# One quarter of s multiplied a pair of products earlier, and four buffers for the gates of att in the last za pair

## The chip, the cores and the metric

The kernel runs on one core of a Trainium2 chip. The metric is the device time of one execution in microseconds (us); the median of the runs shown counts. The core has five engines that run side by side, each in the order of its own instruction list: PE (TensorE: matrix products into PSUM), DVE (VectorE) and ACT (ScalarE: elementwise work), POOL (GpSimd, here mainly an issuer of DMAs) and SP (SyncE, an issuer of DMAs). An instruction that waits holds up whatever stands behind it on its engine; for SP and POOL that is the DMAs queued there.

## The reference

One layer of a streaming encoder with 1024 tokens and a width of 1024. What the change touches is the gate path of the attention branch and the merge of the spatial-gating branch:

```
q, k, v, za, u, vs, zs, gm = split(rmsnorm(x) @ w_in)
a   = window_sink_attention(q, k, v, att_sinks)
a   = (a * silu(za)) @ w_att_out
sgo = chunked_spatial_gating(gelu(u), gelu(vs), ...)
sgo = (sgo * silu(zs)) @ w_sg_out
ga, gs = split(sigmoid(gm + b_merge))
y   = ga * a + gs * sgo
out = rmsnorm(x + y @ w_o)
```

In the kernel's names, `at_dr` holds the attention's result, `a_dr` is `a * silu(za)`, `z_dr` holds `zs` before its silu, `s1_dr` the spatial gating's result that it is multiplied with, and s is their product `silu(zs) * s1`. `gs_dr` and `ga_dr` hold the two halves of `gm`. These are scratch tensors in DRAM, 1024 by 1024 f32.

## The kernel before, in words

**Products.** Every large product is done in pairs of 128-row blocks by `gemm_pair` (from line 345 on): a pair is cut in quarters and made with seven products of half size instead of eight. Each product (`product`, the matmuls of line 342) is 4 times 3 matmuls of 128 by 512, as each f32 operand is split in a high and a low part: ACT casts the high part (`split`, line 155) and DVE subtracts to get the low part (line 156). The right-hand operand is kept as seven forms, named b11, t1, t2, b21, t3, b22, t4 in the order of use; each form has one buffer for its high and one for its low part, so a form for the next stage can be filled once the current stage has used it for the last time. Weights go through `wr` or `s` into `wh` and `wl`, three buffers each (`split_next`). PSUM holds `acc` (tag `ps_mm`), which takes b11, then t2, t3 and t4 on top of one another; between them ACT or DVE must have read it: the copy of line 360 after b11, the copy of line 367 after t2, the subtraction of line 377 after t3. Lines 364, 372 and 381 take the others.

**Hooks.** `gemm_pair` calls a hook after each of its seven products, so other work can be interleaved by hand. The hooks are numbered 1 to 7; (m, h) below is hook h of the pair that begins at block m, with m = 0, 2, 4, 6.

**The za stage.** Four pairs multiply the normalised input's forms with the za weights. Each quarter of a result (`finish`, line 1561) goes through a silu on ACT, and a hook later `finish_silu` multiplies it on DVE (line 1540) with the quarter of att that it gates, `gates.pop(0)`, stores it with a DMA from POOL (line 458) and asks for another gate with `want_gate`, a load of 256 KB from `at_dr` on SP. There are 16 such gates. In this stage they use two buffers, `g0` and `g1`; two gates are asked for at the start and each product asks for the next but one. `finish_silu` runs at hooks 1, 5, 6 and 7, one result behind, and once more after the stage.

**Making s in the shadow of za.** `parts_of_s` (line 1474 on) is a table from (m, h) to steps that prepare the four quarters of s in four buffers `bq0` to `bq3`. A step can load a quarter of `z_dr` (1 MB), apply the silu in place (two ACT instructions, line 1500), load the factors of `s1_dr`, or multiply. Two quarters, those with j = 0, are multiplied with a whole quarter of factors in `bq0` (line 1504). The other two, (1, 1) and (1, 0), are multiplied row by row (line 1511), four rows each, with row loads of 256 KB in buffers `g2` and `g3`. Quarter (1, 0) comes last: its own buffer is `bq0`, which is free only when the second half of quarter (0, 1) has been multiplied at (2, 7). Silus are placed behind the last copy out of PSUM on ACT (`pace`), multiplies behind the last addition on DVE (`term`); these are orders on an engine and not waits. Within such orders and the data's own waits, the compiler's scheduler writes each engine's list.

**The passage to the s stage.** Before the last za pair the first combination of quarters is made (`forms_of`, line 185); after it the forms of s are filled, b11 first. Form b21 is quarter (1, 0); t3 and t4 are combinations, t4 with quarter (1, 0) too. Four gates of `gs_dr` are asked for, in all four buffers, and the s pairs begin; there a gate gets its sigmoid on ACT (line 1574) and multiplies the results on DVE (lines 1581 and 1583).

Of the kernel before, what the change touches and what calls it, by code (L numbers as in the profile page):

```python
# [52 lines left out]
def hybrid_tile(  # L53
# [16 lines left out]
    nc = tc.nc  # L70
# [15 lines left out]
    def mtile(shape, dt, tag, bufs, pool=None):  # L86
        return (pool or main).tile(shape, dt, name=nm(tag), tag=tag, bufs=bufs)

    def scratch(name, shape=(D, S)):
        return dram.tile(list(shape), F32, name=name)  # L90
# [35 lines left out]
    at_dr = scratch("at_dr")  # L126
# [31 lines left out]
    def after(second, first):  # L158

        tc.add_manual_dep(  # L160
            second.ins,
            first.ins.name,
            mybir.DependencyInfo(mybir.DependencyClass.NoSync, mybir.DependencyReason.DATA),
            reason="order",
        )
# [33 lines left out]
    def copy_to(dst, src):  # L199
        nc.sync.dma_start(dst, src)  # L200
# [31 lines left out]
    def half_of(half):  # L232
        return slice(half * HALF, (half + 1) * HALF)
# [96 lines left out]
    term = [None]  # L330
# [20 lines left out]
    def gemm_pair(b, finish, hook=lambda: None, second="o"):  # L351

        n = done[0]
        done[0] += 1
        acc = bank("mm")[:]
        x11, x12, x22 = xtile(), xtile(), xtile()
        product(acc, ready[n, 0], b["b11"], True)
        pace[0] = nc.scalar.copy(x11[:], acc)  # L360
        hook()
        t5 = bank("o")[:]
        product(t5, ready[n, 2], b["t1"], True)
        pace[0] = nc.scalar.mul(x22[:], t5, -1.0)
        hook()
        product(acc, ready[n, 3], b["t2"], False)
        pace[0] = nc.scalar.copy(x12[:], acc)
        split_next()
        hook()
        t2 = bank(second)[:]  # L370
        product(t2, ready[n, 1], b["b21"], True)
        term[0] = term_of_x11[0] = nc.vector.tensor_add(x11[:], x11[:], t2)
        finish(0, 0, x11, x11[:], 1.0)
        split_next()
        hook()
        product(acc, ready[n, 4], b["t3"], False)
        term[0] = nc.vector.tensor_sub(x22[:], x22[:], acc)  # L377
        finish(1, 1, x22, x22[:], 1.0)
        hook()
        product(t5, ready[n, 5], b["b22"], False)  # L380
        term[0] = nc.vector.tensor_add(x12[:], x12[:], t5)
        finish(0, 1, x12, x12[:], 1.0)
        split_next()
        hook()
        product(acc, ready[n, 6], b["t4"], False)
        finish(1, 0, xtile(), acc, -1.0)
        split_next()
        hook()
# [65 lines left out]
    def place(dst, m, half):  # L454
        return dst[m * P : (m + 1) * P, half_of(half)]

    def put(dst, m, half, src, queue=nc.sync):
        queue.dma_start(place(dst, m, half), src)

    def get(src, m, half, bufs, tag="g"):  # L460
        g = mtile([P, HALF], F32, tag, bufs, pool)
        copy_to(g[:], place(src, m, half))
        return g
# [478 lines left out]
    for m in range(0, KC, 2):  # L942

        def finish(i, half, q, src, sign, m=m):
            nc.scalar.activation(q[:], src, AF.Gelu, scale=sign)
            late.append(lambda: mix(m + i, half, q))
# [448 lines left out]
    def bq(n=None):  # L1395
        if n is None:
            n_bq[0] += 1
        return mtile([P, 4, HALF], F32, f"bq{(n_bq[0] if n is None else n) % 4}", 1, pool)
# [47 lines left out]
    def forms_of(qs):  # L1446
        q11, q12, q21, q22 = (qs[k] for k in QUARTERS)
        b = {}

        def fill(name, q):  # L1450
            b.update(new_b((name,)))
            fill_b(b, name, q)

        combine(nc.vector.tensor_sub, q12, q11, q12)
        yield
        fill("b11", q11)
        fill("t1", q12)
        combine(nc.vector.tensor_add, q12, q22, q12)
        fill("t2", q12)
        fill("b21", q21)  # L1460
        combine(nc.vector.tensor_sub, q11, q12, q11)
        fill("t3", q11)
        fill("b22", q22)
        combine(nc.vector.tensor_sub, q21, q12, q21)
        fill("t4", q21)
        yield b

    ORDER = ((0, 0), (1, 1), (0, 1), (1, 0))
    gates = []

    turn = [0]

    def gtag(among=4):
        turn[0] += 1
        return f"g{turn[0] % among}"

    def want_gate(src, m, half, among=4):
        gates.append(get(src, m, half, 1, gtag(among)))

    def parts_of_s():  # L1480

        factors, of_rows = [], {}

        def rows(src, j, half):
            return src[:].rearrange("(c p) t -> p c t", p=P)[:, 4 * j : 4 * j + 4, half_of(half)]

        def load(j, half):
            s_q[j, half] = q = bq()  # L1490
            copy_to(q[:], rows(z_dr, j, half))

        def load_factors(j, half):
            factors.append(bq(0))
            copy_to(factors[-1][:], rows(s1_dr, j, half))

        def silu(j, half):
            for c in range(0, 4, 2):
                v = s_q[j, half][:, c : c + 2, :]
                after(nc.scalar.activation(v, v, AF.Silu), pace[0])  # L1500

        def multiply(j, half, c):
            v = s_q[j, half][:, c : c + 2, :]
            after(nc.vector.tensor_mul(v, v, factors[-1][:, c : c + 2, :]), term[0])

        def load_row(c, half):
            of_rows[c, half] = get(s1_dr, 4 + c, half, 1, f"g{2 + c % 2}")

        def multiply_row(c, half):
            v = s_q[1, half][:, c, :]  # L1510
            after(nc.vector.tensor_mul(v, v, of_rows[c, half][:]), term[0])

        return {
            (0, 1): [(load, 0, 0), (load_factors, 0, 0)],
            (0, 2): [(load, 1, 1)],
            (0, 3): [(load, 0, 1)],
            (0, 4): [(load_row, 0, 1), (load_row, 1, 1)],
            (0, 5): [(silu, 0, 0)],
            (0, 6): [(multiply, 0, 0, 0)],
            (0, 7): [(multiply, 0, 0, 2), (load_factors, 0, 1), (silu, 1, 1)],  # L1520
            (2, 1): [(multiply_row, 0, 1), (multiply_row, 1, 1), (load_row, 2, 1), (load_row, 3, 1)],
            (2, 3): [(silu, 0, 1)],
            (2, 6): [(multiply, 0, 1, 0), (multiply_row, 2, 1)],
            (2, 7): [(multiply, 0, 1, 2), (multiply_row, 3, 1), (load, 1, 0), (load_row, 0, 0), (load_row, 1, 0)],
            (4, 6): [(silu, 1, 0)],
            (4, 7): [(multiply_row, 0, 0), (multiply_row, 1, 0), (load_row, 2, 0), (load_row, 3, 0)],
            (6, 6): [(multiply_row, 2, 0), (multiply_row, 3, 0)],
        }


    of_att = [(m + i, half) for m in range(0, KC, 2) for i, half in ORDER]
    s_q = {}
    making_s = parts_of_s()
    of_za = [0]

    silus = []

    def finish_silu(q, m, half):

        after(nc.vector.tensor_mul(q[:], q[:], gates.pop(0)[:]), term[0])  # L1540
        put(a_dr, m, half, q[:], nc.gpsimd)
        if of_att:
            want_gate(at_dr, *of_att.pop(0), 2)

    def part_of_s(m):
        of_za[0] += 1
        if of_za[0] % 7 not in (2, 3, 4) and silus:
            finish_silu(*silus.pop(0))
        for f, *args in making_s.get((m, (of_za[0] - 1) % 7 + 1), ()):
            f(*args)  # L1550

    for m in range(0, KC, 2):
        if m == 0:
            for _ in range(2):
                want_gate(at_dr, *of_att.pop(0), 2)
        if m == 6:
            s_forms = forms_of(s_q)
            next(s_forms)

        def finish(i, half, q, src, sign):  # L1560
            pace[0] = nc.scalar.activation(q[:], src, AF.Silu, scale=sign)
            silus.append((q, m + i, half))

        gemm_pair(hb, finish, lambda: part_of_s(m), "tp")
    finish_silu(*silus.pop(0))
    for i, half in ORDER:
        want_gate(gs_dr, i, half)
    sb_ = next(s_forms)

    def gate_of(src, m, i, half, col):  # L1570

        g = gates.pop(0)
        c = col + m + i
        gate = nc.scalar.activation(g[:], g[:], AF.Sigmoid, bias=bm_sb[:, c : c + 1])

        after(gate, pace[0])
        return g
# [130 lines left out]
    for p in range(4):  # L1708
        acc = bank("sc" if p < 2 else "mm")[:]
        x11 = mtile([P, HALF], F32, gtag(), 1, pool)  # L1710
        product(acc, ready[N_PAIRS + p, 0], ob["b11"], True)
        nc.scalar.copy(x11[:], acc)
        accs.append(acc)
        firsts.append(x11)
# [185 lines left out]
```

## Time and profile before

| what | us |
|---|---|
| median of 3 runs | 914.42 (913.27 to 915.49) |
| the profiled execution, whole | 915.36 |
| its span, first to last instruction | 913.6 |
| busy in the span: PE, DVE, ACT, POOL | 895.3, 696.7, 527.1, 141.9 |
| mean granted clock of TensorE | 0.995 |

The profile is of one execution. The span is what the trace covers; the execution's own time is 1.8 us longer. Times in rows are us from the start of the span, L and a number is a line of the kernel. In a timeline row stand start, duration, engine, line, operation, output<-inputs, shapes, count, and in brackets how long the engine was idle before and what ended that. In the chain of waits each row is a start, a duration and what the end of the program hung on in that time. PE's matmuls overlap, so that their durations add up to more than the time.

### The profile page before, as it was taken

The numbers are of one execution on the slowest core, as the hardware profiler recorded it, in microseconds if no ns is written. First come the engines' busy times: TensorE is split into PE (matmuls) and PEld (weight loads), VectorE is DVE, ScalarE is ACT, GpSimd is POOL, SyncE is SP. The second block draws the span as 40 slices with busy tenths as digits, with TensorE's granted clock in tenths as the row PEclk, the third lists the DMA queues.
The fourth block names the chain that finished last, engine by engine and source line by source line (L and its number), as shares of the span: only waits on it lengthen the run. The fifth ranks groups of instructions, "written<-read, shape, count | busy, mean of one in ns | idle before, by whom it ended". The sixth has DMA issues, their size and how long they took to land.

```text
span 913.6 us, 13183 instructions
## 1 busy us (share of the span) xinstructions
PE 895.3 (98%) x4284; PEld 745.1 (82%) x4284; DVE 696.7 (76%) x1263; ACT 527.1 (58%) x1058; POOL 141.9 (16%) x204
## 2 busy tenths in 40 slices
PE   8999999999999899999999999999998999999996
PEld 6778888888888788888888888888877887888885
DVE  6869966666685678888878888647797589579996
ACT  6866533334544467677677676664674385367443
POOL 1222222212030001111110111201001111110012
PEclk9999999999999999999999999999999999999999
DMA  9997888958788657878686789899859755998632
GB/s 330 204 248 212 271 203 173 172 158 257 260 258 274 199 167 212 212 153 208 180 227 228 234 240 229 215 338 343 304 195 363 224 201 150 312 304 277 208 117 113
DMA packets 131598, 209.57 MB, mean 229 GB/s; under 512 B 12649, under 2 KB 61033, under 8 KB 131530
## 3 DMA queue, kind: packets, MB, share of 16 engines
q1 hardware_dynamic: 110072, 149.74, 49.7%
q0 software_dynamic: 21312, 58.73, 28.3%
q8 instruction: 34, 0.56, 0.3%
q14 instruction: 34, 0.28, 0.1%
q10 hardware_dynamic: 146, 0.27, 0.1%
HBM read 147.74 MB, written 86.11 MB: 256 GB/s over the span
## 4 chain that ended last, share of the span: by engine, by line
PE 88%; DVE 7%; DMA 2%; issue 1%; ACT 1%; SPq 0%; DVEq 0%; ACTq 0%
PE ps_mm L342 37%; PE ps_o L342 27%; PE ps_sc L1230 3%; PE ps_mm L669 3%; PE ps_tp L342 3%; PE ps_tp L669 2%; PE ps_o L1315 2%; PE ps_sc L342 2%; PE ps_tp L1274 2%; PE ps_o L669 2%; PE ps_tp L917 2%; PE ps_sc L669 1%; DVE bq L185 1%; DVE wl L156 1%; DMA wr<-in_w_dram 1%
## 5 line engine op out<-in xcount | busy, mean ns | idle before, releaser
L155 ACT CAST wh<-s 128x1024 fp32r<-128x1024 f32 (+1 forms) x79 | 79.2, 1005 | 90.2 <-PE ps_mm L342 48.6
L156 DVE TENSOR_TENSOR wl<-wr,wh 128x512 fp32r<-128x512 f32 (+1 forms) x77 | 72.0, 936 | 51.3 <-ACT wh L155 50.7
L156 DVE TENSOR_TENSOR wl<-s,wh 128x1024 fp32r<-128x1024 f32 (+1 forms) x79 | 92.5, 1171 | 10.8 <-ACT wh L155 10.6
L155 ACT CAST wh<-wr 128x512 fp32r<-128x512 f32 (+1 forms) x77 | 63.1, 821 | 62.6 <-PE ps_mm L342 34.2
L342 PE MATMUL ps_o<-T_t1h,wh 128*128 128x512 f32 x148 | 58.9, 398 | 0.8 <-ACT wh L155 0.7
L342 PE MATMUL ps_o<-T_b22h,wh 128*128 128x512 f32 x148 | 58.2, 393 | 0.0
L342 PE MATMUL ps_o<-T_b22l,wh 128*128 128x512 f32 x148 | 57.9, 391 | 0.0
L342 PE MATMUL ps_o<-T_b22h,wl 128*128 128x512 f32 x148 | 57.8, 390 | 0.0
L342 PE MATMUL ps_mm<-T_b11h,wl 128*128 128x512 f32 x140 | 54.9, 392 | 2.8 <-DVE wl L156 2.8
L342 PE MATMUL ps_o<-T_t1h,wl 128*128 128x512 f32 x148 | 57.7, 390 | 0.0
L342 PE MATMUL ps_o<-T_t1l,wh 128*128 128x512 f32 x148 | 57.6, 389 | 0.0
L342 PE MATMUL ps_mm<-T_t4h,wh 128*128 128x512 f32 x140 | 55.5, 397 | 1.2 <-DVE x L377 1.2
L342 PE MATMUL ps_mm<-T_t2h,wl 128*128 128x512 f32 x140 | 55.2, 395 | 0.0
L342 PE MATMUL ps_mm<-T_t3l,wh 128*128 128x512 f32 x140 | 54.6, 390 | 0.6 <-DVE T_t3l L156 0.6
L342 PE MATMUL ps_mm<-T_t2l,wh 128*128 128x512 f32 x140 | 55.2, 394 | 0.0
L342 PE MATMUL ps_mm<-T_t4h,wl 128*128 128x512 f32 x140 | 55.1, 394 | 0.0
L342 PE MATMUL ps_mm<-T_b11h,wh 128*128 128x512 f32 x140 | 55.1, 393 | 0.0
L342 PE MATMUL ps_mm<-T_t4l,wh 128*128 128x512 f32 x140 | 55.0, 393 | 0.0
L342 PE MATMUL ps_mm<-T_t2h,wh 128*128 128x512 f32 x140 | 55.0, 393 | 0.0
L342 PE MATMUL ps_mm<-T_b11l,wh 128*128 128x512 f32 x140 | 54.9, 392 | 0.0
L342 PE MATMUL ps_mm<-T_t3h,wh 128*128 128x512 f32 x140 | 54.9, 392 | 0.0
L1243 ACT ACTIVATE pr<-ps_sc,sm 128x192 f32<-128x192 f32 (+2 forms) x128 | 50.9, 410 | 6.6 <-DVE sm L1239 5.5
(389 smaller groups left out, 2397.4 us busy)
## 6 DMA issues: line engine op xcount, KB each, us to landing
wr<-in_w_dram SPq DMA_DIRECT2D x86, 256.0 KB
sums<-in_w_dram POOLq DMA_DIRECT2D x20, 512.0 KB, 6.5
s<-sums SPq DMA_DIRECT2D x20, 512.0 KB
q_hl<-qhl SPq DMA_DIRECT2D x16, 512.0 KB
q<-q_hl SPq DMA_DIRECT2D x64, 128.0 KB
y_dr<-x POOLq DMA_DIRECT2D x28, 256.0 KB, 6.7
g<-in_w_dram POOLq DMA_DIRECT2D x12, 512.0 KB, 6.7
wr<-in_w_dram SPq DMA_DIRECT2D x11, 512.0 KB
```

The costliest lines, as they stand in the source:

```text
L155: nc.scalar.copy(hi, src)
L156: return nc.vector.tensor_sub(lo, src, hi.bitcast(F32))
L185: op(dst[:, i : i + 2, :], a[:, i : i + 2, :], c[:, i : i + 2, :])
L342: nc.tensor.matmul(acc, lt, rt, start=fresh and k == 0 and n == 0, stop=k == 3 and n == 2, skip_group_check=True,)
L669: mm = nc.tensor.matmul(acc[:], lt, rt, start=fresh and k == 0 and n == 0, stop=k == 3 and n == 2, skip_group_check=True,)
L917: nc.tensor.matmul(pm[:, t * P : (t + 1) * P], xh[:, half * 4 + t, g * P : (g + 1) * P], bias[-1][1][:, g % 4, :], start=True, stop=True,)
L1230: nc.tensor.matmul(sc[:, i, k0:], q_of[:, c, i * P : (i + 1) * P], kt[:, f, k0:], start=f == 0, stop=f == 1,)
L1243: nc.scalar.activation(held_in[c, i], sc[:, i, lo:hi], AF.Exp, bias=nmax[:, c, i : i + 1], scale=-1.0, accum_out=sums[:, c, i : i + 1],)
L1274: nc.tensor.transpose(dst, pr[:, i, block * P : block * P + width], ident[:])
L1315: nc.tensor.matmul(po[:, cs], lt, rt, start=n == 0, stop=n == len(terms) - 1)
```

## The change

A list `free_tags` takes the place of the counter that named the gates' buffers. It begins with `g0` and `g1`; a gate takes the first free name and gives it back when it is used. At the start of the last za pair (m = 6) `g2` and `g3` are added and two more gates are asked for. For that, row loads in `g2` and `g3` have to be through: the steps for quarter (1, 0) are moved in the table.

| step for quarter (1, 0) | before | after |
|---|---|---|
| load of the quarter, loads of rows 0 and 1 | (2, 7) | (2, 7) |
| silu | (4, 6) | (4, 2) |
| multiplies of rows 0 and 1, loads of rows 2 and 3 | (4, 7) | (4, 3) |
| multiplies of rows 2 and 3 | (6, 6) | (4, 6) |

```diff
-    turn = [0]
-
-    def gtag(among=4):
-        turn[0] += 1
-        return f"g{turn[0] % among}"
-
-    def want_gate(src, m, half, among=4):
-        gates.append(get(src, m, half, 1, gtag(among)))
+    free_tags = ["g0", "g1"]
+
+    def gtag():
+        tag = free_tags.pop(0)
+        free_tags.append(tag)
+        return tag
+
+    def want_gate(src, m, half):
+        tag = free_tags.pop(0)
+        gates.append((tag, get(src, m, half, 1, tag)))
+
+    def next_gate():
+        tag, g = gates.pop(0)
+        free_tags.append(tag)
+        return g
...
-            (4, 6): [(silu, 1, 0)],
-            (4, 7): [(multiply_row, 0, 0), (multiply_row, 1, 0), (load_row, 2, 0), (load_row, 3, 0)],
-            (6, 6): [(multiply_row, 2, 0), (multiply_row, 3, 0)],
+            (4, 2): [(silu, 1, 0)],
+            (4, 3): [(multiply_row, 0, 0), (multiply_row, 1, 0), (load_row, 2, 0), (load_row, 3, 0)],
+            (4, 6): [(multiply_row, 2, 0), (multiply_row, 3, 0)],
...
-        after(nc.vector.tensor_mul(q[:], q[:], gates.pop(0)[:]), term[0])
+        after(nc.vector.tensor_mul(q[:], q[:], next_gate()[:]), term[0])
         put(a_dr, m, half, q[:], nc.gpsimd)
         if of_att:
-            want_gate(at_dr, *of_att.pop(0), 2)
+            want_gate(at_dr, *of_att.pop(0))
...
-        if m == 0:
+        if m in (0, 6):
+            if m:
+                free_tags += ["g2", "g3"]
             for _ in range(2):
-                want_gate(at_dr, *of_att.pop(0), 2)
+                want_gate(at_dr, *of_att.pop(0))
...
-        g = gates.pop(0)
+        g = next_gate()
```

## The prediction

> **What bounds the kernel now.** I read the page first, then the chain of waits, then each engine's timeline from 592 to 745 us, where the four za pairs and the first s pair lie.
>
> ```profile
> span 913.6 us, 13183 instructions
> ...
> PE 88%; DVE 7%; DMA 2%; issue 1%; ACT 1%; SPq 0%; DVEq 0%; ACTq 0%
> ```
>
> PE holds 88% of the chain, so time is won or lost where PE stands still or runs at a lower clock. The chain of waits leaves PE once near the change, at the passage from the za pairs to the s pairs:
>
> ```profile
> 670.78 5.11 DMA g<-at_dr
> ...
> 690.36 1.15 DVE wl L156
> 691.51 0.04 issue
> 691.55 6.90 PE ps_mm L342 x22
> ```
>
> Up to 691.55, where PE resumes, the chain runs through DVE, which prepares the forms of s and the next weights for PE, and through one DMA: the last gate of att, issued at 670.78, 5.11 us. The same in DVE's timeline (start, duration, line, out<-in, idle time before):
>
> ```profile
> 657.95 2.36 DVE L156 TENSOR_TENSOR T_t1l<-bq,T_t1h 128x1024 fp32r<-128x1024 f32 x2 [0.36 <-ACT T_t1h L155]
> 670.64 1.29 DVE L1511 TENSOR_TENSOR bq<-bq,g 128x512 f32<-128x512 f32 x2
> 675.98 0.69 DVE L1540 TENSOR_TENSOR x<-x,g 128x512 f32<-128x512 f32 x1 [1.01 <-DMA g<-at_dr]
> ```
>
> After 657.95 DVE has hardly an idle moment up to 691.5. In it stand the two row multiplies of line 1511 (1.29 us) and one idle time of 1.01 us, for that gate. What PE loses by it is in the table of windows (PE busy, PEld, DVE, ACT, POOL, clock, DMA share, GB/s):
>
> ```profile
> 680.67:698.29 17.62, 14.51 (x54) 10.67 (x54) 16.76 (x19) 9.89 (x12) 1.62 (x3) 0.90 0.81 294
> 689.20:692.57 3.37, 1.63 (x6) 1.03 (x7) 3.37 (x5) 0.45 (x1) 0.17 (x1) 1.00 1.04 377
> 692.57:695.98 3.41, 3.41 (x9) 2.63 (x8) 3.41 (x6) 0.00 (x0) 1.45 (x3) 0.50 1.07 392
> 764.00:778.00 14.00, 12.84 (x56) 9.98 (x54) 13.06 (x16) 5.89 (x7) 3.51 (x4) 1.00 0.49 132
> ```
>
> In 17.62 us PE is busy for 14.51, so 3.1 us are idle, 1.74 of them in the 3.37 us before 692.57. Then the granted clock is 0.50 for 3.41 us, which costs half of that, 1.7 us.
>
> **The change part by part.** (a) The multiplies of rows 2 and 3 of quarter (1, 0) leave hook 6 of the last za pair (670.64) for hook 6 of the pair before (about 648). (b) The silu of that quarter moves from hook 6 to hook 2 of that pair, its first two row multiplies from hook 7 to hook 3, and with them the loads of rows 2 and 3. (c) Buffers g2 and g3, free by then, take two att gates at the start of the last pair. (d) Buffer names come from a free list, which elsewhere gives the same first-in, first-out order. No instruction is added or removed; all are moved.
>
> **Gain on DVE.** The two multiplies take 1.29 us out of the full stretch. The wait of 1.01 us goes too. SP now issues the 15th gate at 666.14 and the 16th at 670.78, each when the product two before has freed one of two buffers:
>
> ```profile
> 666.14 0.33 SPq L200 DMA_DIRECT2D g<-at_dr  x1
> ```
>
> With four buffers gates 14 and 15 go out when g2 and g3 come free, and the last one behind the 12th product at 652.88; all three have over 10 us before their use after 670, twice the 5.11 us that the chain shows for the last. So DVE can be 2.3 us earlier at 691.5. ACT bounds this from below:
>
> ```profile
> 678.98 1.05 ACT L155 CAST T_t3h<-bq 128x1024 fp32r<-128x1024 f32 x1 [2.96 <-DVE bq L185]
> 679.93 0.58 ACT L367 COPY x<-ps_mm 128x512 f32<-128x512 f32 x1
> ```
> ```profile
> 639.87 0.39 PE L342 MATMUL ps_tp<-T_b21h,wh 128*128 128x512 f32 x1
> ```
> ```profile
> 677.95 0.39 PE L342 MATMUL ps_tp<-T_b21h,wh 128*128 128x512 f32 x1
> ```
>
> ACT waits 2.96 us for DVE at 678.98 and is then never idle until the next wait of the passage. The copy at 679.93 (line 367) follows the t2 product, after which PE starts b21 at 677.95; two pairs earlier the same copy comes at 640.37 (row below), half a microsecond behind b21's start at 639.87, so this one can move 1.5 us. The casts around it can pass it, since the written order goes by readiness. Bounds 1.5 and 2.3 us; I take 2.2, nearer to DVE's row, the one the chain names.
>
> PE would then resume at 691.55 - 2.2 = 689.35. It also reaches that wait earlier: the stalls ahead of it (3.1 - 1.74 = 1.4 us) shrink as well. A single stop of 1.6 to 1.9 us is left, about as long as now, so I leave the half-clock stretch where it is.
>
> The Trainium skill (TensorE: Matmul & The Clock Gate, "What's actually happening") says that the clock is halved after at least one idle window of about 3.4 us. The length of the stretch agrees with it, the cause does not: here 1.74 idle us in 3.37 were enough. By the page's rule there would be no half-speed stretch either before or after and nothing to win from it; by the rows, 1.7 us.
>
> **Cost of the early silu.** The quarter is loaded at 637.07, after the multiply that frees its buffer; this load isn't moved:
>
> ```profile
> 608.74 3.04 SPq L200 DMA_DIRECT2D g<-at_dr  x2
> 637.07 0.37 SPq L200 DMA_DIRECT2D bq<-z_dr  x1
> ```
> ```profile
> 637.34 0.60 ACT L364 ACTIVATE x<-ps_o 128x512 f32<-128x512 f32 x1 [2.13 <-PE ps_o L342]
> 639.84 0.62 ACT L155 CAST wh<-wr 128x512 fp32r<-128x512 f32 x1 [1.90 <-PE ps_mm L342]
> 640.37 0.58 ACT L367 COPY x<-ps_mm 128x512 f32<-128x512 f32 x1
> 646.23 0.63 ACT L1561 ACTIVATE x<-x 128x512 f32<-128x512 f32 x1 [2.09 <-DVE x L377]
> 649.53 2.00 ACT L1500 ACTIVATE bq<-bq 128x1024 f32<-128x1024 f32 x2
> ```
>
> Hook 2 lies at 637.34 (the line 364 scaling), so the silu may be queued any time after 637.9. Its 1 MB isn't there yet. Bounds from the nearest rows: the gate issued last of the two from 608.74 on ended waits of DVE at 619.56 and after, behind 1 MB loads, and the one issued at 649.54 (second of two) at 652.88:
>
> ```profile
> 619.56 1.36 DVE L1540 TENSOR_TENSOR x<-x,g 128x512 f32<-128x512 f32 x2 [0.60 <-DMA g<-at_dr]
> 652.88 0.69 DVE L1540 TENSOR_TENSOR x<-x,g 128x512 f32<-128x512 f32 x1 [0.42 <-DMA g<-at_dr]
> 630.60 0.69 DVE L1540 TENSOR_TENSOR x<-x,g 128x512 f32<-128x512 f32 x1 [0.73 <-ACT x L1561]
> 632.35 1.22 DVE L1504 TENSOR_TENSOR bq<-bq,bq 128x1024 f32<-128x1024 f32 x1
> ```
> ```profile
> 646.82 3.05 SPq L200 DMA_DIRECT2D g<-at_dr  x2
> ```
> ```profile
> 620.67 0.43 SPq L200 DMA_DIRECT2D bq<-s_dr  x1
> ```
>
> That is 3.3 to 10.8 us, so the quarter lands between 640.4 and 647.9. The order that the compiler wrote narrows it. ACT works in order, and behind a silu that waits stand the copy at 640.37, the casts of the next pair's weights and the silus of za. Where it is queued decides. The order seems to know how late loads are: the multiply at 632.35 needs the 1 MB issued at 620.67, and DVE idled 0.73 us before 630.60 without it, so it was not expected before 630, over 9 us after its issue. The same 9 us after 637.07 give 646, my estimate of the landing, and the silu lies beside the za silu at 646.23. There ACT has 2.09 us of idle time before and the 2.00 us that the silu leaves free at 649.53, and the cost is nothing. If that cover is gone the price is that of the rivals: bounds 0 and 8.4 us (arrival at 647.9, ahead of the copy).
>
> The Trainium skill (DMA: Bandwidth & Descriptors, "Anatomy of one DMA — SWDGE (gpsimd) path") fits 2.0 us plus bytes over 436 GB/s, an estimate of 4.4 us for 1 MB, with the landing at 641.5. By that the silu would wait for almost nothing wherever it is queued; the gates above took up to 10.8 us for a quarter of the bytes.
>
> **The moved loads and multiplies.** The first two row multiplies need half of the silu, so they run near 647 instead of 651.17, beside these:
>
> ```profile
> 642.59 0.39 PE L342 MATMUL ps_mm<-T_t3h,wh 128*128 128x512 f32 x1
> 648.02 0.39 PE L342 MATMUL ps_mm<-T_t4h,wh 128*128 128x512 f32 x1
> ```
> ```profile
> 645.50 0.69 DVE L377 TENSOR_TENSOR x<-x,ps_mm 128x512 f32<-128x512 f32 x1 [0.63 <-PE ps_mm L342]
> 651.17 1.28 DVE L1511 TENSOR_TENSOR bq<-bq,g 128x512 f32<-128x512 f32 x2
> 655.23 2.36 DVE L156 TENSOR_TENSOR T_b11l<-bq,T_b11h 128x1024 fp32r<-128x1024 f32 x2 [0.53 <-ACT T_b11h L155]
> ```
>
> Line 377 at 645.50 frees the bank that PE's t4 product (648.02) adds into; it must not be late by more than 1.8 us. After them SP issues rows 2 and 3, near 648.4 instead of 651.98:
>
> ```profile
> 651.98 0.86 SPq L200 DMA_DIRECT2D g<-s_dr  x2
> ```
>
> At 3.3 to 10.8 us they land at 651.7 to 659.2. Up to 655.23 the two multiplies fit in the room left by line 1511 at 651.17 and the idle 0.53: no cost. If they land after 657.95 they fall into the full stretch and 1.3 us of the gain is gone. The nearest row, 649.54, gives 3.3 us, so I count nothing. Loads queued behind them on SP (the gates, the sums of weights) keep number and size and two gates move from 666 and 670 to about 654.
>
> **Sum.** Against the profiled execution: 913.6 us span plus 1.8 around it is 915.36, and 0.9 above the median of 914.42. It loses 2.2, with costs of nothing: 913.2 there, 912.2 on the median.
>
> **Rivals.** *The clock stays up.* If the stop is under some 1.2 us, or is cut by another order of the products, the 0.50 stretch goes. For: the passage at 764 to 778, of the same build, has 1.16 us idle (14.00 - 12.84) and a clock of 1.00. Against: I count a stop of 1.6 or more. 912.2 - 1.7 = 910.5.
>
> *The row multiplies stop DVE.* If the first two stand ahead of line 377, this waits for half the silu (646 + 1.0), two multiplies (1.28) and its own 0.69: done at 649.0, and t4 starts 1.0 us late, 3.0 if the next weights' cast is ahead too. 912.2 + 1.0 to 3.0: 913.2 to 915.2, about no change. For: they have the earlier place in the program. Against: they are ready only after 645.50.
>
> *The rows come late*, behind the sums on SP as the row at 651.98 would be, and the stretch keeps its 1.3 us: 913.5.
>
> *Slower: the silu is queued ahead of the copy at 640.37.* The copy must be done before PE's t3 product at 642.59, which adds to the bank it reads. With the load landing at L it is done at L + 2.00 + 0.53 + 0.58, so PE stands from L = 639.5 on, and from L = 641.7 the gain is used up. At L = 646, 6.5 us late: 912.2 + 6.5 = 918.7; at 644, 916.7. For: the program places it at hook 2, ahead of the copy. Against: the order at 632.35.
>
> **How the numbers follow.** Forecast 0.33; clock stays up 0.22; DVE stopped 0.15; rows late 0.14; slower 0.16. A difference counts from 0.2%, 1.8 us. Faster: 0.26 of the forecast (its own range, 911.5 to 913.2, reaches past 912.6), 0.22, and 0.04 from the rows' case, 0.52. Slower: 0.16 and 0.03 from the stopped DVE, 0.19. No change: the rest, 0.29. The range runs from 909.6 (2.3 gained, the clock up, a further 0.8 of stop gone) to 917.0; it leaves out the upper 0.10 of the slow case and little below.
>
> **What would show it.** Right: no idle DVE before line 1540 near 674, no line 1511 after 657, PE resuming about 2 us sooner than 691.55, the silu of line 1500 starting near 646. The clock: a 0.50 stretch after the passage or none. Wrong: a stop of PE near 642 or 648; ACT idle ahead of line 1500; row loads issued after 651; or a passage in which ACT's casts, not DVE, are what PE waits for.

## The result and the profile after

The changed kernel takes 915.65 us (median of 22 runs, 913.67 to 918.36) where the kernel before takes 913.99 in the same series (22 runs, 911.70 to 915.53): the ratio is 1.002, with a 95% interval of 1.0013 to 1.0028. It is slower by a little; the forecast was faster. The profiled execution of the changed kernel took 917.38 us, against 915.36 for that of before.

```profile
span 915.6 us, 13184 instructions
```

Lines from 1471 on have moved: the silu of a quarter is now L1507, the multiplies of a quarter L1511, the row multiplies L1518, the za multiply L1547, the za silu L1570. The matmuls and the lines up to 381 keep their numbers.

The passage from za to s, the place that the change is for, is better. The table of windows (length, then busy time of PE, PEld, DVE, ACT, POOL, then clock, DMA share, GB/s) after:

```profile
649.17:652.39 3.22, 0.00 (x1) 0.00 (x0) 2.11 (x4) 1.33 (x3) 0.00 (x0) 1.00 0.47 163
653.16:656.58 3.42, 3.42 (x9) 2.65 (x8) 3.32 (x5) 1.31 (x2) 1.08 (x2) 0.50 0.77 244
680.67:698.29 17.62, 16.45 (x72) 12.98 (x71) 17.62 (x20) 11.34 (x14) 1.01 (x2) 1.00 0.87 328
```

In the third row PE is idle for 1.17 us where it was 3.11 before, and the clock is 1.00 throughout. But the first two rows are new, 40 us ahead of the passage: PE does nothing for 3.22 us, and 0.77 us later its clock is halved for 3.41. PE's timeline names the place, between the last product of b22 and the first of t4 in the third za pair:

```profile
648.78 0.39 PE L342 MATMUL ps_o<-T_b22h,wl 128*128 128x512 f32 x1
652.39 0.50 PE L342 MATMUL ps_mm<-T_t4h,wh 128*128 128x512 f32 x1 [3.22 <-DVE x L377]
...
695.18 0.50 PE L342 MATMUL ps_mm<-T_b11h,wl 128*128 128x512 f32 x1 [0.94 <-DVE wl L156]
```

The last row is the longest stop that is left at the passage, 0.94 us. The chain of waits shows how the new stop comes about (start, duration, what the end hung on):

```profile
637.23 9.69 DMA bq<-z_dr
...
647.02 2.01 ACT bq L1507 x2
649.03 0.52 ACT x L1570
649.55 0.94 ACT wh L155
...
650.51 0.04 DVE wl L156
...
651.66 0.69 DVE x L377
...
652.39 1.87 PE ps_mm L342 x5
```

Read from the top: the load of quarter (1, 0) takes 9.69 us; the silu has been waiting for it; behind the silu stand the za silu and the cast `wh` of the next weights; behind the cast stands its low part on DVE; behind that L377, which frees the bank that t4 adds into. ACT's and DVE's timelines, with the idle time in brackets:

```profile
641.35 0.58 ACT L367 COPY x<-ps_mm 128x512 f32<-128x512 f32 x1
647.02 2.01 ACT L1507 ACTIVATE bq<-bq 128x1024 f32<-128x1024 f32 x2 [5.09 <-DMA bq<-z_dr]
648.93 0.61 ACT L1570 ACTIVATE x<-x 128x512 f32<-128x512 f32 x1
649.45 1.03 ACT L155 CAST wh<-wr 128x1024 fp32r<-128x1024 f32 x1
```
```profile
648.12 1.29 DVE L1518 TENSOR_TENSOR bq<-bq,g 128x512 f32<-128x512 f32 x2 [3.66 <-ACT bq L1507]
650.51 1.23 DVE L156 TENSOR_TENSOR wl<-wr,wh 128x1024 fp32r<-128x1024 f32 x1 [1.11 <-ACT wh L155]
651.66 0.68 DVE L377 TENSOR_TENSOR x<-x,ps_mm 128x512 f32<-128x512 f32 x1
```

In the kernel before the same cast ran 6.9 us earlier in the trace (5.9 if counted from the first za pair, which begins 1.0 us later in the changed kernel's trace). What it waited for was PE's b21 product, as the bracket says, and no load:

```profile
642.56 1.06 ACT L155 CAST wh<-wr 128x1024 fp32r<-128x1024 f32 x1 [1.61 <-PE ps_tp L342]
```

The account, counted from one matmul's start to the next beyond the usual 0.227 us: the third pair lost nothing and now loses 5.08 (3.38 of stop, 1.7 of half clock); the passage lost 5.78 (1.7 of them half clock) and now loses 1.72. That is +5.08 - 4.06 = +1.0; and in this execution the first za pair began 1.0 us later than in that of before, work which the change does not touch. Together they are the 2.0 us between the two spans. The medians differ by 1.66. That this is so near is in part luck, as the second 1.0 us is scatter: over the ten profiles of this document the first za pair begins between 592.2 and 594.7.

### The profile page after: what moved, and what is told of

It reads as the page before. It is cut to its first block, busy times and chain, and to the rows that moved or that the text cites. A ratio compares the mean times of both kernels' runs of the same rounds, so it can differ in the third digit from the quotient of the medians.

```text
span 915.6 us, 13184 instructions
## 1 busy us (share of the span) xinstructions
PE 896.0 (98%) x4284; PEld 745.9 (81%) x4284; DVE 696.4 (76%) x1263; ACT 527.2 (58%) x1058; POOL 141.3 (15%) x204
## 4 chain that ended last, share of the span: by engine, by line
PE 84%; DVE 8%; DMA 3%; issue 2%; ACT 2%; SPq 0%; DVEq 0%; ACTq 0%
PE ps_mm L342 35%; PE ps_o L342 26%; PE ps_sc L1230 3%; PE ps_mm L669 3%; PE ps_tp L669 2%; PE ps_o L1315 2%; PE ps_sc L342 2%; PE ps_tp L1274 2%; PE ps_tp L342 2%; PE ps_o L669 2%; PE ps_tp L917 2%; DVE wl L156 1%; DVE bq L185 1%; PE ps_sc L669 1%; DMA bq<-z_dr 1%
## 5 line engine op out<-in xcount | busy, mean ns | idle before, releaser
L342 PE MATMUL ps_mm<-T_t3h,wl 128*128 128x512 f32 x140 | 54.7, 390 | 0.0
```

Source lines behind the costliest of these rows:

```text
L342: nc.tensor.matmul(acc, lt, rt, start=fresh and k == 0 and n == 0, stop=k == 3 and n == 2, skip_group_check=True,)
```

## The experiments

The theory after the profile: the load lands 5 us after the place at which the written order has its silu, and the engines, which keep their order, pass this on through the cast to L377 and t4. The rival: the two row multiplies ahead of L377 are what stops t4. Each table below stands in place of the changed kernel's; ratios are to the kernel before, on the same chip in the same series. The changed kernel's 1.002 is of an earlier series; the first four experiments share one series and the last four another.

### The silu later: e1_silu_hook4

```diff
-            (4, 2): [(silu, 1, 0)],
-            (4, 3): [(multiply_row, 0, 0), (multiply_row, 1, 0), (load_row, 2, 0), (load_row, 3, 0)],
-            (4, 6): [(multiply_row, 2, 0), (multiply_row, 3, 0)],
+            (4, 4): [(silu, 1, 0)],
+            (4, 5): [(multiply_row, 0, 0), (multiply_row, 1, 0), (load_row, 2, 0), (load_row, 3, 0)],
+            (4, 7): [(multiply_row, 2, 0), (multiply_row, 3, 0)],
```

> The silu of quarter (1, 0) two hooks later than in the change, at (4, 4), its first two row multiplies at (4, 5), the last two at (4, 7); four gate buffers in the last pair as in the change. Theory (early silu): what the change loses is only that ACT waits 5.1 us for the quarter's load with the cast of the next weights behind it; here the silu stands behind the za silus of (0, 0) and (1, 1), so PE has no stop in the third za pair, and the passage to s stays as short as after the change (1.7 us of lost PE time instead of 5.8): about 4 us under before, ratio 0.9945 to 0.997. Rival (the passage was short only because PE came late to it): the passage goes back to 4 us or more of lost time and the ratio is 0.998 to 1.000. Rival (multiplies): they stop DVE here as well, ahead of line 381, and PE stops by 1 us or more in the third pair.

Measured: 911.86 us (12 runs), ratio 0.997 (0.9959 to 0.9981). ACT's timeline and the windows:

```profile
643.61 1.05 ACT L155 CAST wh<-wr 128x1024 fp32r<-128x1024 f32 x1 [1.61 <-PE ps_tp L342]
644.57 0.62 ACT L1570 ACTIVATE x<-x 128x512 f32<-128x512 f32 x1
645.75 2.01 ACT L1507 ACTIVATE bq<-bq 128x1024 f32<-128x1024 f32 x2 [0.56 <-DMA bq<-z_dr]
```
```profile
640.00:660.00 20.00, 20.00 (x90) 16.56 (x89) 15.44 (x19) 13.39 (x18) 2.16 (x4) 1.00 0.94 321
680.00:697.00 17.00, 15.82 (x69) 12.47 (x68) 17.00 (x19) 10.02 (x13) 2.17 (x4) 1.00 0.87 314
```

The cast is ahead of the silu again, PE is busy for all of the 20 us round the old stop, and the passage keeps what the change gave it: 1.18 us idle, clock 1.00. So the gain at the passage does not come from the delay ahead of it, and this version is faster than both kernels. The ratio is at the slow end of what was expected: the two profiles' passages differ by the 4 us of the theory, the medians by 2.7.

### The multiplies later, the silu as in the change: e2_rows_late

```diff
-            (4, 3): [(multiply_row, 0, 0), (multiply_row, 1, 0), (load_row, 2, 0), (load_row, 3, 0)],
-            (4, 6): [(multiply_row, 2, 0), (multiply_row, 3, 0)],
+            (4, 6): [(multiply_row, 0, 0), (multiply_row, 1, 0), (load_row, 2, 0), (load_row, 3, 0)],
+            (4, 7): [(multiply_row, 2, 0), (multiply_row, 3, 0)],
```

> The silu stays at (4, 2) as in the change, but the first two row multiplies go to (4, 6) and the last two to (4, 7). Theory (the cast behind the silu): DVE's line 377 waits for the low part of the next weights, that for the cast on ACT, that for the silu and its load; so PE's stop ahead of t4 in the third pair stays at 3 us or more with the half-speed stretch behind it, and the time is that of the change, ratio to before 1.000 to 1.003. Rival (the multiplies ahead of line 377 stop DVE, as the prediction had it): the stop falls under 1.5 us, the half-speed stretch goes, and the ratio is 0.995 to 0.998.

Measured: 918.05 us (9 runs), ratio 1.0042 (1.0028 to 1.0057), more than expected. ACT's timeline, and then DVE's, where nothing stands ahead of L377 now but the cast's low part:

```profile
644.61 2.01 ACT L1507 ACTIVATE bq<-bq 128x1024 f32<-128x1024 f32 x2 [4.69 <-DMA bq<-z_dr]
646.53 0.61 ACT L1570 ACTIVATE x<-x 128x512 f32<-128x512 f32 x1
647.04 1.03 ACT L155 CAST wh<-wr 128x1024 fp32r<-128x1024 f32 x1
```
```profile
648.11 1.22 DVE L156 TENSOR_TENSOR wl<-wr,wh 128x1024 fp32r<-128x1024 f32 x1 [5.66 <-ACT wh L155]
649.25 0.68 DVE L377 TENSOR_TENSOR x<-x,ps_mm 128x512 f32<-128x512 f32 x1
```

t4 starts at 649.98: 5.37 us after the silu, just as in the changed kernel (652.39 - 647.02), where the two multiplies are between. They cost nothing there, since the cast is what DVE waits for in the end; the rival falls. The stop here is 2.97 us with half a clock behind it, and the passage loses 2.8 us in place of 1.72: DVE waits 1.41 us at 659.25 for a load of the rows moved back, and one of their multiplies, at 660.99, falls into the stretch in which DVE is never idle. The profiled execution is the fastest of the nine (916.06), so it does not show all of what the median lost.

### The table without the two more gates: e3_table_only

```diff
-        if m in (0, 6):
-            if m:
-                free_tags += ["g2", "g3"]
+        if m == 0:
...
+    free_tags += ["g2", "g3"]
     for i, half in ORDER:
```

> The change's table, but two gate buffers to the end of the za stage as before. Theory (both parts shorten the passage): the stop of 3.4 us in the third pair stays; in the passage DVE waits for the last gate again, about 1 us, so PE loses 2.5 to 4.5 us there instead of 1.7, and the time is 1 to 3 us over the change's: ratio to before 1.003 to 1.005. Rival (the gates don't matter, the moved multiplies did it): as the change, 1.001 to 1.003.

Measured: 918.76 us (6 runs), ratio 1.0052 (1.0034 to 1.0069). In its profile t4 stops for 2.71 us, again 5.37 us behind the silu (644.86 to 650.23), and there is half a clock both there and at the passage, which loses 4.7 us:

```profile
694.60:698.00 3.40, 3.40 (x9) 2.63 (x9) 3.40 (x6) 0.00 (x0) 1.47 (x3) 0.51 1.04 387
```

With two buffers the passage keeps most of its old loss, and the ratio is 0.0032 or 2.9 us above the changed kernel's 1.002: with this table the two more gates are worth that.

### The gates without the table: e4_gates_only

```diff
+        def more_gates():
+            free_tags.extend(("g2", "g3"))
+            for _ in range(2):
+                want_gate(at_dr, *of_att.pop(0))
...
-            (4, 2): [(silu, 1, 0)],
-            (4, 3): [(multiply_row, 0, 0), (multiply_row, 1, 0), (load_row, 2, 0), (load_row, 3, 0)],
-            (4, 6): [(multiply_row, 2, 0), (multiply_row, 3, 0)],
+            (4, 6): [(silu, 1, 0)],
+            (4, 7): [(multiply_row, 0, 0), (multiply_row, 1, 0), (load_row, 2, 0), (load_row, 3, 0)],
+            (6, 1): [(multiply_row, 2, 0), (multiply_row, 3, 0), (more_gates,)],
...
-        if m in (0, 6):
-            if m:
-                free_tags += ["g2", "g3"]
+        if m == 0:
```

> Silu at (4, 6) and first row multiplies at (4, 7) as before; the last two row multiplies at (6, 1) instead of (6, 6), and then four gate buffers. Nothing waits for the quarter's load early, and the two multiplies stay inside DVE's full stretch. Theory (both parts): no stop in the third pair; the 1.0 us wait for the last gate goes and 1.3 us of multiplies stay, so the passage loses 1 us less: ratio 0.998 to 0.9995, and 1.7 us less again if the half-speed stretch goes too. Rival (the gates don't matter): ratio 0.9995 to 1.0005.

Measured: 916.21 us (12 runs), ratio 1.0015 (1.0001 to 1.0029), a miss. DVE's and PE's timelines show one new loss:

```profile
658.69 1.29 DVE L1523 TENSOR_TENSOR bq<-bq,g 128x512 f32<-128x512 f32 x2 [3.02 <-DMA g<-s_dr]
...
667.92 0.68 DVE L377 TENSOR_TENSOR x<-x,ps_mm 128x512 f32<-128x512 f32 x1
```
```profile
668.65 0.50 PE L342 MATMUL ps_mm<-T_t4h,wh 128*128 128x512 f32 x1 [2.20 <-DVE x L377]
...
692.16 0.50 PE L342 MATMUL ps_mm<-T_b11h,wl 128*128 128x512 f32 x1 [1.73 <-DVE wl L156]
```

L1523 is the row multiply here. DVE stands for 3.02 us at the loads of rows 2 and 3, which were issued at 651.30 and landed at 658.7; the forms of s and L377 of the fourth pair queue behind, and t4 of that pair stops for 2.36 us from start to start. It is the changed kernel's fault in another place: an instruction that waits for a load was put ahead of one that PE needs. The gates did in this profile what was expected of them: the passage loses 3.1 us, against 4.1 of stops in the kernel before, and here no half clock comes on top. The profiled execution (914.37 us) is faster than the median, and in it 2.36 lost and some 2.7 won at the passage come out even. What the median lost beyond that no profile shows. Half-speed stretches behind these two stops in other executions are the likely cause: the twelve runs reach from 913.84 us at a mean clock of 0.999 to 918.81 at 0.993.

### The cast first, the multiplies ahead of L377: e5_cast_first

```diff
+        if rows_first:
+            after(term[0], rows_first.pop())
...
+            (4, 4): [(silu, 1, 0), (multiply_row, 0, 0), (multiply_row, 1, 0), (load_row, 2, 0), (load_row, 3, 0)],
```

The first two lines stand behind L377; `rows_first` holds the second row multiply. The last line takes the place of the lines for (4, 2) and (4, 3).

> The silu of quarter (1, 0) stands behind the cast of the next weights on ScalarE, and the multiplies of rows 0 and 1 are kept ahead of L377 (the subtraction that frees the bank of t4) by an order of their own; gates as in the changed kernel. The theory (the stop of t4 came through the cast that stood behind the silu: silu 2.0, cast 1.0, low part 1.2 behind the load that lands at 646.9): the cast runs at about 642.6 again; the multiplies wait for the silu and L377 comes at about 649.4, so t4 stops for 0.7 to 1.4 us in place of 3.38 and the clock stays at 1.00 behind it; the passage from za to s keeps its 1.7 us of loss; ratio to the kernel before 0.996 to 0.9995. The rival (the two multiplies alone are what held t4): a stop of 3 us or more, half the clock behind it, ratio 1.001 or more.

Measured: 912.12 us (11 runs), ratio 0.9982 (0.9971 to 0.9993). The timelines of DVE (L1511 is the silu here, L1522 the row multiply and L379 the old L377) and of PE:

```profile
643.24 1.23 DVE L156 TENSOR_TENSOR wl<-wr,wh 128x1024 fp32r<-128x1024 f32 x1 [0.17 <-ACT wh L155]
647.21 1.29 DVE L1522 TENSOR_TENSOR bq<-bq,g 128x512 f32<-128x512 f32 x2 [2.75 <-ACT bq L1511]
648.43 0.68 DVE L379 TENSOR_TENSOR x<-x,ps_mm 128x512 f32<-128x512 f32 x1
```
```profile
649.16 0.50 PE L342 MATMUL ps_mm<-T_t4h,wh 128*128 128x512 f32 x1 [1.38 <-DVE x L379]
```

With the multiplies alone between the silu and L377, t4 starts 3.04 us after the silu (646.12 to 649.16) in place of 5.37, PE idles 1.38 us in place of 3.22, and the clock stays up. Counted from start to start the stop is 1.54, a little over the expected 1.4.

### Work for PE in the stop: e6_keep_warm

Twelve products that nothing reads are added to the changed kernel, between b22 and t4:

```diff
+        def keep_warm(n):
+            warm, v = bank("sc"), hb["b11"][0]
+            for _ in range(n):
+                nc.tensor.matmul(warm[:], v[:, 0, 0:P], v[:, 0, :], start=True, stop=True)
...
+            (4, 6): [(keep_warm, 12), (multiply_row, 2, 0), (multiply_row, 3, 0)],
```

> The changed kernel with twelve products of hb's first block into an unused bank, written between b22 and t4 of the third za pair: they do 2.7 us of work that nothing reads in the stop of 3.38 us. The theory (behind the stop the clock is granted at 0.50 for 3.41 us because TensorE stood idle, and that is a price of its own of 1.7 us): t4 starts as late as in the changed kernel, about 3.4 us late, but the granted clock stays at 1.00 behind it, and the kernel is 1.3 to 1.9 us faster than the changed one, ratio to the kernel before 0.9995 to 1.001. The rival (the half clock has nothing to do with the idle time, or comes out of it anyway): half the clock for 3.41 us again and a ratio of 1.0013 or more.

Measured: 914.22 us (11 runs), ratio 1.0003 (0.9991 to 1.0015). PE's timeline, and the window behind the stop:

```profile
646.61 2.88 PE L1523 MATMUL ps_sc<-T_b11h 128*128 128x512 f32 x12
650.60 0.50 PE L342 MATMUL ps_mm<-T_t4h,wh 128*128 128x512 f32 x1 [1.10 <-DVE x L377]
```
```profile
650.60:656.20 5.60, 5.60 (x24) 4.61 (x25) 5.27 (x8) 3.62 (x5) 1.28 (x3) 1.00 0.75 256
```

t4 is as late as ever, 5.38 us behind the silu (645.22), and later than it would follow b22 by 650.60 - 646.61 = 3.99 us, but the clock stays at 1.00. Against the changed kernel's 1.002 that is 0.0017 or 1.6 us, near the 1.7 us that the clock in the changed kernel's profile gives for the half-speed stretch. The two intervals just overlap, so the 1.7 us is the firmer number.

### The better table with two gates: e7_table4_two_gates

The table of e1_silu_hook4 with the edit of e3_table_only.

> The table that puts the silu at the fourth call of the third pair, rows 0 and 1 at the fifth and rows 2 and 3 at the seventh, but with two buffers for the gates of att in the last za pair as before (g2 and g3 join the list ahead of the gates of gs). The theory (stop and passage are separate; the gates from four buffers are worth the wait for the last gate at the passage, about 1.0 to 1.2 us, and with it the stretch at half clock, 1.7 us): no stop in the third pair, 2.7 to 4.7 us lost at the passage against 1.73 with four buffers; ratio to the kernel before 0.998 to 1.0005, that is 0.001 to 0.003 above the same table with four. The rival (the gates are worth nothing, the rows alone shorten the passage): 1.7 us lost at the passage and a ratio of 0.997.

Measured: 912.31 us (11 runs), ratio 0.9977 (0.9965 to 0.9989), a little faster than expected. No stop in the third pair. DVE's timeline, and the windows at the passage:

```profile
677.13 0.69 DVE L1547 TENSOR_TENSOR x<-x,g 128x512 f32<-128x512 f32 x1 [1.34 <-DMA g<-at_dr]
```
```profile
688.98:692.40 3.42, 1.56 (x6) 0.99 (x7) 3.42 (x5) 0.86 (x1) 0.00 (x0) 1.00 1.03 364
692.40:695.81 3.41, 3.41 (x10) 2.64 (x9) 3.41 (x6) 0.00 (x0) 1.63 (x3) 0.50 1.04 389
```

The wait for the last gate is back, 1.34 us, and the profiled passage loses 4.94 us, 1.7 of them by the clock. But that execution was the slowest of the eleven (915.44). The ratio is only 0.0007 above e1_silu_hook4's and the intervals overlap: with this table the wait is shown, but its price is not settled.

### The load earlier: e8_load_earlier

The silu stays ahead of the cast; the load goes out earlier, since the products that free its buffer are asked for earlier:

```diff
-            (2, 6): [(multiply, 0, 1, 0), (multiply_row, 2, 1)],
-            (2, 7): [(multiply, 0, 1, 2), (multiply_row, 3, 1), (load, 1, 0), (load_row, 0, 0), (load_row, 1, 0)],
-            (4, 2): [(silu, 1, 0)],
-            (4, 3): [(multiply_row, 0, 0), (multiply_row, 1, 0), (load_row, 2, 0), (load_row, 3, 0)],
+            (2, 5): [(multiply, 0, 1, 0)],
+            (2, 6): [(multiply, 0, 1, 2), (load, 1, 0), (multiply_row, 2, 1)],
+            (2, 7): [(multiply_row, 3, 1), (load_row, 0, 0), (load_row, 1, 0)],
+            (4, 3): [(silu, 1, 0)],
+            (4, 4): [(multiply_row, 0, 0), (multiply_row, 1, 0), (load_row, 2, 0), (load_row, 3, 0)],
```

> The silu stays ahead of the cast on ScalarE, as in the changed kernel, with the multiplies of rows 0 and 1 behind it; but the two products of quarter (0, 1), whose factors give up the buffer that the load of quarter (1, 0) goes to, are asked for one call earlier in the second pair, so that this load is issued some 3 us earlier. The theory (the stop is the late landing, passed on by the engines in their written order): t4's stop shrinks by as much as the landing moves, from 3.38 us to 0 to 1 us where the load lands by 644, without half a clock behind it; the passage keeps its 1.7; ratio 0.995 to 0.9985. The rival (the place of the silu costs the stop whatever the load does): 3 us or more lost again.

Measured: 911.77 us (12 runs), ratio 0.9982 (0.9969 to 0.9996). The timelines of SP's queue and of ACT:

```profile
632.86 0.37 SPq L200 DMA_DIRECT2D bq<-z_dr  x1
```
```profile
641.11 2.01 ACT L1507 ACTIVATE bq<-bq 128x1024 f32<-128x1024 f32 x2 [0.99 <-DMA bq<-z_dr]
643.02 1.03 ACT L155 CAST wh<-wr 128x1024 fp32r<-128x1024 f32 x1
```

Issued 4.4 us earlier in the trace, the load landed at 641.0, 5.9 earlier. This execution reached the first za pair 1.8 us earlier (592.80 against 594.61), so counted from there it is 2.6 and 4.1 us. ACT waits 0.99 us for it and t4's stop is 0.25 us. The silu and the first row multiplies are asked for one hook later than in the change, but on ACT the silu still stands ahead of the cast: with that order kept, the stop shrank with the landing.

## Why the prediction was wrong, step by step

**The gain at the passage was right, and larger than forecast.** The stops there fell from 4.1 us to 1.72, by 2.4 (forecast 2.2): no line 1518 in the stretch after 661, no wait of DVE for a gate. What was missed is the clock: the prediction took a single stop of 1.6 to 1.9 us to be left, and left the half-speed stretch in place. The longest is 0.94 us, the clock stays at 1.00, and 1.7 us more are gained. That was the rival *the clock stays up*, at this place.

**The cost of the early silu is the step that failed.** It was set at nothing: "The order seems to know how late loads are", so that the silu would lie beside the za silu at 646.23. The landing was estimated well, 646 against 646.92 measured, though one of its bounds was misread: the 10.8 us belong to the first of the two gates issued from 608.74 on, and the second went out at 611.46. The order did not know it: it has the silu right behind the copy of line 367, five microseconds early, ahead of the cast. The row at 632.35, on which the step rested, showed an instruction that came late, but nothing in it tells a load that was thought late from a place in the program that was late. The program asks for that multiply at (2, 6), right behind the za multiply that ran at 630.60; its place alone is enough for the row. The cost is 3.38 us of stop and 1.7 of clock.

**The rival that named the chain.** *The row multiplies stop DVE* gave 1.0 us, "3.0 if the next weights' cast is ahead too". The second is what happened, at 3.38, but with the cast alone as the cause (e2_rows_late); the first is e5_cast_first, with 1.54. Two things were wrong in it: its chance of 0.15, and that its price held no half clock behind a stop of three microseconds, though 1.74 idle us had one in the rows of before. With it, 912.2 + 3.0 + 1.7 = 916.9; less the 1.7 won back at the passage, 915.2.

**The slower rival**, the silu ahead of the copy, did not come: the copy ran at 641.35, before the wait.

**Rows 2 and 3 cost nothing**, as forecast: in the changed kernel's timelines SP issued their loads at 648.84 and DVE ran the two multiplies at 655.19, ahead of the stretch that PE waits for.

```profile
648.84 0.92 SPq L200 DMA_DIRECT2D g<-s_dr  x2
```
```profile
655.19 1.28 DVE L1518 TENSOR_TENSOR bq<-bq,g 128x512 f32<-128x512 f32 x2
```

So the forecast's 2.2 us were there, with 1.7 more, and 5.1 were lost at a place whose cost was taken as nothing.

## What to carry to other kernels

Where engines work in a written order, the place of an instruction that waits for a load matters as much as the load: before moving one forward, list what stands behind it on its engine up to PE, and price the move with the landing time of that very load in the trace. The cheap cure is to put the wait behind the last thing that PE needs soon (e1_silu_hook4, two hooks later), or to issue the load earlier (e8_load_earlier). And a stop of PE of some two microseconds is to be priced with a half clock behind it, which came in most cases here, though not where the grid of the next section cut the stop in two.

## What was not expected of the hardware

**Half-speed stretches begin on a fixed grid.** Two more windows of the changed kernel's profile:

```profile
318.66:322.07 3.41, 3.41 (x12) 2.65 (x11) 2.23 (x9) 3.03 (x14) 0.00 (x0) 0.50 0.92 202
649.75:653.16 3.41, 0.77 (x3) 0.67 (x4) 2.65 (x4) 1.52 (x3) 0.00 (x0) 1.00 0.53 178
```

From the stretch that starts at 318.66 to the one at 653.16 are 334.5 us, 98 times 3.413. In all nine profiles with more than one such stretch (that of e6_keep_warm has one) the starts are whole multiples of 3.413 us apart (the last of each lies at the kernel's end, from 903 us on), and the grid lies differently to the kernel's start in each. The Trainium skill (TensorE: Matmul & The Clock Gate, "What's actually happening") has a free-running window of 3413 ns, and the traces agree with that. It also asks for an idle window, and there they differ: between 640 and 900 us, every window of the grid with 1.74 us or more without a matmul was followed by half speed (six cases, 1.74 to 2.64) and none with 1.38 or less was. What counts there is the idle time inside one window, as e4_gates_only shows, whose stop of 2.20 us (666.45 to 668.65) is cut by the border at 667.27 and costs no clock; nor does its stop of 1.73 us at the passage, which the border at 691.17 cuts:

```profile
663.86:667.27 3.41, 2.59 (x12) 1.82 (x10) 3.41 (x5) 1.51 (x3) 0.00 (x0) 1.00 0.45 154
667.27:670.69 3.42, 2.04 (x9) 1.70 (x10) 3.42 (x5) 3.42 (x6) 0.54 (x1) 1.00 0.33 100
670.69:674.10 3.41, 3.41 (x17) 2.83 (x16) 3.41 (x5) 3.41 (x6) 1.07 (x2) 1.00 0.52 165
```

Between 300 and 320 us it does not sort so cleanly: windows with 1.20 to 1.65 us idle were followed by half speed in some profiles and others with 1.51 to 1.70 were not; what decides there stays open.

**So the same kernel wins or loses whole stretches from run to run.** One is 3.41 x 0.5 = 1.7 us and takes 0.0019 off the mean granted clock. Of 35 runs of the kernel before in the second series, the five at a clock of 0.998 took 912.0 us on average and the sixteen at 0.994 and 0.995 took 915.2. It is the likely reason why single profiles and medians differ by a microsecond or two (e7_table4_two_gates above); one profiled execution shows one throw of it.
